# Dividing attention outputs instead of probabilities by the softmax sums, and moving six steps of a modulation vector one sub-layer ahead

## The chip, the core and the metric

The kernel runs on one core of a Trainium2 chip. The metric is the device time of one execution in microseconds (us), as a median over runs. The core has five engines that run side by side and meet at semaphores: PE (TensorE, matmuls; PEld is its weight loading), DVE (VectorE), ACT (ScalarE), POOL (GpSimd) and SP (SyncE, which here only issues DMAs). Each engine takes its own instructions strictly in order.

## The reference

Two layers of a decoder on 256 tokens of width 1024. Each layer is a half-step SwiGLU, a token mixer, and another half-step SwiGLU. Layer 0 mixes with the forgetting attention ("fox"), layer 1 with the dilated attention ("dil"). Each of the six sub-layers begins with an RMS norm that is shifted and scaled, and ends with a gate; shift, scale and gate are vectors computed from `c`.

```python
mod = (silu(c) @ mod_w[i] + mod_b[i]).reshape(B, 3, 3, D)    # 3 sub-layers x (shift, scale, gate)
...
h = modulate(rms_norm(x, norm_g[i, 1]), shift[:, 1], scale[:, 1])
...
# fox, for each of 16 heads of 64, queries in two blocks of 128:
logits = q @ k.T * scale + cum[q] - cum[k]          # masked causally
p = softmax(logits)                                  # exp(logits - max) / sum
o = p @ v
# dil, three groups of windows, merged by their softmax sums, so that one softmax runs over all of them
...
x = x + gate[:, 1] * (o @ w_out)
```

## The kernel before, in words

Everything is computed on two token tiles of 128 (`t` = 0, 1). Weights come in as f32, and each weight tile (128 x 1024) is split into two parts: ACT rounds it (`wh`, L206), DVE subtracts (`wl`, L215). A product is then three matmuls (`mm3`, L394 to L396, or `mm_blocks`, L389 to L391). PE's and SP's instructions stand in the order in which the program text emits them; those of DVE, ACT and POOL are ordered by a scheduler when the kernel is built.

The text walks through the weight tiles and calls `tick()` about every 1.4 us of PE work. At a tick, `weights.advance()` splits further tiles ahead of their use, and events that were booked with `at(delay, fn)` fall due, in order of their tick. Attention is emitted in this way, between the projections' matmuls.

**Attention** (`attention`, L902) handles a group of four heads in eight steps (head `i`, token tile `t`). `scores` emits the logits on PE, the row maximum on DVE (`lo`, `nm`, L916) and the exponential on ACT (L918), which also adds up the rows into `sums`. One tick later `share` (L922) takes the reciprocal of a sum (L926) and multiplies the row's probabilities by it (L927), both on DVE. `turn` (L929) then transposes the probabilities on PE (L935), ACT copies them to `pt` (L937), and `values` (L940) multiplies them with `v` into one PSUM bank `ob` (L948), in which the heads' outputs stand transposed. `close` (L950) splits `ob` into `oTh` (ACT) and `oTl` (DVE, L954), the operands of the output projection. There are four groups in fox and four in dil; in the last one of dil, `close` runs once for each token tile.

**Modulation vectors** (`Mods`, L256). A vector of 1024 is computed in eight steps, each of which loads 512 KB of `mod_w` into one of two buffers `mraw` and multiplies and adds it into `acc` on DVE (L296). After the eighth step the vector is split and summed over the partitions by matmuls with ones (L346, L348), into one of three tiles `mod0` (shift), `mod1` (scale), `mod2` (gate). A `Pump` (L361) spreads a sub-layer's steps evenly over its weight tiles; what is left is emitted in `flush` (L378), just ahead of the last four tiles of the output projection. In the first SwiGLU (`ffnA`) 24 steps run: its own gate and the shift and scale of fox. In fox another 24 run, the first eight of them for fox's gate.

**Boundary** (L414). At the end of a sub-layer DVE multiplies a token tile's output by the gate (`gy`, L431), adds it to `x` (L435), multiplies by the next scale (`u`, L451), and, after ACT's squares and POOL's root (`rs`, L411), finishes the next input (L460), which PE transposes (L469) for the next sub-layer. Two token tiles follow each other, and PE fills in the other's matmuls meanwhile.

**Fox** also computes the forget gates' running sums: from the `v` projection's extra columns DVE and ACT make `fl` (L1051 to L1070), which PE sums up (L1081) into `ncum` before the first logits.

Of the kernel before, what the change touches and what calls it, by code (L numbers as in the profile page):

```python
# [9 lines left out]
F32 = mybir.dt.float32  # L10
# [7 lines left out]
P = 128  # L18
# [35 lines left out]
LAST_CUTS = (0, 512, 768, 1024)  # L54
PUMP_FFN = 48
PUMP_FOX = 32
PUMP_DIL = 80
# [5 lines left out]
AHEAD = 5  # L63
SHARE = 1
QUIET0 = 5
# [26 lines left out]
def trunk_kernel(ctx, tc, x_in, c_in, positions, mod_w, mod_b, norm_g, w_gate, w_up, w_down,  # L92
# [163 lines left out]
    class Mods:  # L256
# [30 lines left out]
        def run(self):  # L287
# [12 lines left out]
            if k == 0:  # L300
                self.bias(self.done - 1 + KT)
            elif k == 2:
                dst = main.tile([P, D], F32, tag=f"mod{j}", name=f"mod{j}")
                if j == 1:
                    nc.sync.dma_start(dst, dram(norm_g, (l * 3 + s) * D, [[0, P], [1, D]]))
                mods[v] = dst
            elif k == KT - 1:
                self.finish(v, acc)

        def finish(self, v, acc):  # L310
# [50 lines left out]
    class Pump:  # L361


        def __init__(self, vectors, units):
            self.n, self.units, self.done, self.seen = len(vectors) * KT, units, 0, 0

        def __call__(self):
            self.seen += 1
            self.go(min(self.n, -(-self.n * self.seen // self.units)))

# [7 lines left out]
        def flush(self):  # L378
            while self.done < self.n or vectors.open:
                self.go(self.n)  # L380
                tick()
# [206 lines left out]

    def ffn(l, i, s, pool, n_first, new_mods, permute=False, opening=None):
        pump = Pump(new_mods, PUMP_FFN)  # L590
        weights.spare = pool, 1, "xwh", "xwl"
# [310 lines left out]
    def attention(g, first, gap, delays, pv_first, logits, mask, vblk, oTh, oTl, done, pool, width, pts_n, by_tile=False):  # L902
# [18 lines left out]

        def share(i, t):  # L922

            n, _ = mask(t)
            ri = pool.tile([P, 1], F32, tag="ri", bufs=4, name="ri")
            dve.reciprocal(ri, sums[:, t, i:i + 1])  # L926
            dve.tensor_scalar(pts[i, t][:, 0:n], pts[i, t][:, 0:n], ri, None, op0=OP.mult)  # L927

        def turn(i, t):  # L929
# [19 lines left out]

        def close(ts):  # L950
            ks = slice(2 * g, 2 * g + 2)
            for t in range(ts.start, ts.stop):
                act.copy(oTh[t][:, ks, :], ob[0][:, :, t, :])
                dve.tensor_sub(oTl[t][:, ks, :], ob[0][:, :, t, :], oTh[t][:, ks, :].bitcast(F32))  # L954
                done.update(((2 * g, t), (2 * g + 1, t)))

        for s, (i, t) in enumerate(steps):
            base = first + s * gap
            at(base, lambda i=i, t=t: scores(i, t))
            at(base + SHARE, lambda i=i, t=t: share(i, t))  # L960
            at(base + delays[0], lambda i=i, t=t: turn(i, t))
            end = max(pv_first + s * gap, base + sum(delays))
            if i % 2:
                at(end, lambda i=i, t=t: values(i, t))
            if by_tile and i == HG - 1:
                at(end, lambda t=t: close(slice(t, t + 1)))
# [66 lines left out]
    def fox(l, pool, n_first):  # L1033
        pump = Pump(MODS_FOX, PUMP_FOX)
        weights.spare = pool, 2, "qs", "ks"
# [3 lines left out]
        oTl = [pool.tile([P, KT, P], F32R, tag=f"oTl{t}", name=f"oTl{t}") for t in range(NT)]  # L1039
        fl = pool.tile([P, NT, CUM], F32, name="fl")  # L1040
        nc.gpsimd.memset(fl, 0.0)
# [81 lines left out]
        def do_heads(g):  # L1123
            attention(g, FOX_FIRST[g], 1, (T_FOX, PV_FOX), 0, *heads(g, *qkT[g]), oTh, oTl, done, pool, S, 6)

# [240 lines left out]
    with tc.tile_pool(name="ffnA", bufs=1) as fp:  # L1366
        vectors.start()
        spread_out(12, fox_tables())
        ffn(0, 0, 0, fp, 0, MODS_A, opening=opening)
    with tc.tile_pool(name="fox", bufs=1) as ap:  # L1370
# [42 lines left out]
```

## Time and profile before

| what | value |
|---|---|
| median of 3 runs | 1244.7 us (1244.12 to 1245.76) |
| the profiled execution's own time | 1244.32 us |
| span of its trace | 1242.3 us |
| mean granted PE clock | 0.996 of full speed |
| instructions in the trace | 21040 |

The trace covers the span from the first to the last instruction; the execution's own time is 2.0 us longer. Rows of the trace are in a section below. In each, a line such as L927 is the line of the code above, `out<-in` are the tiles, `x32` is a count, and what stands behind a bar or in brackets is the idle time of the engine before these instructions and what ended it.

### The profile page before, as it was taken

Reading aid. Unit: us, or ns where it says so; the run is one execution under the profiler, and the core shown is the slowest. Engines: PE = TensorE matmul, PEld = TensorE weight load, DVE = VectorE, ACT = ScalarE, POOL = GpSimd, SP = SyncE. Lnnn points to the kernel's source line nnn. Section 1 sums busy time; section 2 is a strip of 40 time slices with the busy share of each in tenths; the row PEclk is TensorE's granted clock in tenths of the full one; section 3 lists DMA queues with packets and bytes.
Section 4 is the critical chain, followed back from the end, with each engine's and each line's share of the span. In section 5 each row is a group of like instructions: output and inputs, shape, how many; then the busy total and the mean of one; then the engine's idle time right before and its main releaser. Section 6 shows DMA issues by size and latency. Waiting matters only on the chain.

```text
span 1242.3 us, 21040 instructions
## 1 busy us (share of the span) xinstructions
PE 1208.2 (97%) x8098; PEld 1082.3 (87%) x8098; DVE 965.5 (78%) x1452; ACT 660.6 (53%) x1000; POOL 96.4 (8%) x124
## 2 busy tenths in 40 slices
PE   5999999978999999999999999999999999999998
PEld 5999988866779999889999888878788787999987
DVE  7879777999988888569987669988787877765653
ACT  4446444667754555444554436566565655544440
POOL 1000000212010000000000003121131200000000
PEclk8999999999999999999999999999999999999999
DMA  9879885785749988638888647746545652867561
GB/s 334 277 271 333 284 329 159 227 277 169 228 132 317 342 275 323 207 117 285 294 289 316 214 153 237 223 158 208 176 152 171 202 172 85 270 207 220 169 207 47
DMA packets 152067, 281.18 MB, mean 226 GB/s; under 512 B 13424, under 2 KB 79504, under 8 KB 151968
## 3 DMA queue, kind: packets, MB, share of 16 engines
q1 hardware_dynamic: 151968, 279.85, 67.9%
q8 instruction: 63, 1.03, 0.3%
q14 instruction: 36, 0.29, 0.1%
HBM read 277.71 MB, written 2.10 MB: 225 GB/s over the span
## 4 chain that ended last, share of the span: by engine, by line
PE 86%; DVE 6%; ACT 2%; issue 2%; DMA 2%; POOL 1%; SPq 0%; POOLq 0%; DVEq 0%; ACTq 0%
PE bank L394 14%; PE bank L395 13%; PE bank L396 13%; PE block_bank L391 13%; PE block_bank L389 12%; PE block_bank L390 12%; PE obank L948 1%; DVE wl L215 1%; PE bank L935 1%; PE bank L1293 1%; POOL hrs L860 1%; PE bank L1288 1%; DVE acc L296 1%; PE bank L469 1%; PE bank L346 1%
## 5 line engine op out<-in xcount | busy, mean ns | idle before, releaser
L215 DVE TENSOR_TENSOR wl<-raw,wh 128x1024 fp32r<-128x1024 f32 (+1 forms) x360 | 434.9, 1215 | 156.2 <-ACT wh L206 152.7
L206 ACT CAST wh<-raw 128x1024 fp32r<-128x1024 f32 (+1 forms) x360 | 374.4, 1046 | 316.9 <-PE bank L396 118.1
L389 PE MATMUL block_bank<-hTh,wh 128*128 128x256 f32 x1312 | 371.8, 283 | 3.3 <-ACT hTh L783 3.3
L391 PE MATMUL block_bank<-hTh,wl 128*128 128x256 f32 x1312 | 371.6, 283 | 0.0
L390 PE MATMUL block_bank<-hTl,wh 128*128 128x256 f32 x1312 | 370.6, 282 | 0.0
L389 PEld LDWEIGHTS block_bank<-hTh,wh 128*128 128x128 f32 x1312 | 248.5, 189 | 3.7 <-ACT hTh L783 3.4
L390 PEld LDWEIGHTS block_bank<-hTl,wh 128*128 128x128 f32 x1312 | 248.1, 189 | 0.5 <-DVE hTl L786 0.2
L391 PEld LDWEIGHTS block_bank<-hTh,wl 128*128 128x128 f32 x1312 | 247.8, 189 | 0.0
L394 PE MATMUL bank<-wh,hTh 128*128 128x512 f32 (+2 forms) x496 | 191.1, 385 | 0.0
L396 PE MATMUL bank<-wh,hTl 128*128 128x512 f32 (+2 forms) x496 | 181.9, 367 | 0.0
L395 PE MATMUL bank<-wl,hTh 128*128 128x512 f32 (+2 forms) x496 | 181.7, 366 | 0.0
L296 DVE SCALAR_TENSOR_TENSOR acc<-mraw,ccols,acc 128x1024 f32<-128x1024 f32 x112 | 143.2, 1279 | 20.1 <-DMA mraw<-in_mod_w_dram 19.7
L395 PE MATMUL bank<-wl,aTh 128*128 128x512 f32 (+1 forms) x420 | 146.4, 349 | 0.0
L394 PE MATMUL bank<-wh,aTh 128*128 128x512 f32 (+1 forms) x420 | 146.1, 348 | 0.0
L396 PE MATMUL bank<-wh,aTl 128*128 128x512 f32 (+1 forms) x420 | 145.7, 347 | 0.0
L396 PEld LDWEIGHTS bank<-wh,hTl 128*128 128x128 f32 x496 | 93.6, 189 | 16.7 <-DVE hTl L471 0.5
L394 PEld LDWEIGHTS bank<-wh,hTh 128*128 128x128 f32 x496 | 93.8, 189 | 15.9 <-issue 1.0
L395 PEld LDWEIGHTS bank<-wl,hTh 128*128 128x128 f32 x496 | 94.0, 189 | 12.2
L394 PEld LDWEIGHTS bank<-wh,aTh 128*128 128x128 f32 x420 | 79.5, 189 | 10.9
L396 PEld LDWEIGHTS bank<-wh,aTl 128*128 128x128 f32 x420 | 79.3, 189 | 10.5
L395 PEld LDWEIGHTS bank<-wl,aTh 128*128 128x128 f32 x420 | 79.5, 189 | 10.1
L918 ACT ACTIVATE lo<-lo,nm 128x128 f32<-128x128 f32 (+1 forms) x64 | 37.8, 591 | 39.8 <-DVE nm L916 39.2
(215 smaller groups left out, 1304.4 us busy)
## 6 DMA issues: line engine op xcount, KB each, us to landing
mraw<-in_mod_w_dram SPq DMA_DIRECT2D x128, 512.0 KB, 5.1
raw<-in_ffn_w_down_dram SPq DMA_DIRECT2D x88, 512.0 KB, 3.7
raw<-in_ffn_w_gate_dram SPq DMA_DIRECT2D x76, 512.0 KB, 4.1
raw<-in_ffn_w_up_dram SPq DMA_DIRECT2D x76, 512.0 KB, 4.7
raw<-in_dil_w_in_dram SPq DMA_DIRECT2D x128, 256.0 KB, 4.1
raw<-in_fox_w_in_dram SPq DMA_DIRECT2D x36, 256.0 KB, 5.0
oraw<-in_mod_w_dram SPq DMA_DIRECT2D x32, 256.0 KB, 6.4
raw<-in_ffn_w_gate_dram SPq DMA_DIRECT2D x24, 256.0 KB, 5.1
```

What stands on the lines that cost most here:

```text
L206: act.copy(wh, self.raws[self.hi])
L215: dve.tensor_sub(wl, self.raws[self.lo], wh.bitcast(F32))
L296: dve.scalar_tensor_tensor(acc, raw, ccol[:, k:k + 1], self.bias_tile if k == 0 else acc, op0=OP.mult, op1=OP.add)
L346: pe.matmul(bp, ones, ah, start=True, stop=al is None)
L389: pe.matmul(out_i, wh[:, blk], hTh[:, :, k, :], start=first and i % 2 == 0, stop=False)
L390: pe.matmul(out_i, wh[:, blk], hTl[:, :, k, :], start=False, stop=False)
L391: pe.matmul(out_i, wl[:, blk], hTh[:, :, k, :], start=False, stop=last and i % 2 == 1)
L394: pe.matmul(o, ah, wh, start=first, stop=False)
L395: pe.matmul(o, ah, wl, start=False, stop=False)
L396: pe.matmul(o, al, wh, start=False, stop=last)
L469: pe.transpose(tp[:, k, :], self.u[h][:, k * P:(k + 1) * P], ident)
L918: act.activation(lo[:, 0:n], lo[:, 0:n], AF.Exp, bias=nm, scale=-1.0, accum_out=sums[:, t, i:i + 1])
```

## The change

`share` is gone: the exponentials go to `turn` and `values` undivided. `close` takes one reciprocal for the whole group, lets ACT spread it over 64 columns for each head (`wide`, 128 x 512), and one tick later `normalize` transposes that on PE (32 transposes in all, four for each group) into a bank `rbank`, copies it to `on` (ACT), multiplies `ob` by it (DVE), and splits `on` into `oTh` and `oTl` as before. `wide` uses the buffer of the norm's squares (`sq`), and in fox `on` that of `fl`. In fox one buffer of `pt` goes (6 to 5).

Six of the eight steps of fox's gate vector move to `ffnA`: its pump runs 30 steps over 58 units (24 over 48 before), and fox's 18 over 32. So that the gate of `ffnA` isn't overwritten, a vector's tile is now taken at its last step.

```diff
+PUMP_A = 58
+MORE_A = 6
...
-SHARE = 1
+RI_DELAY = 1
...
-        def __init__(self, vectors, units):
-            self.n, self.units, self.done, self.seen = len(vectors) * KT, units, 0, 0
+        def __init__(self, vectors, units, more=0, less=0):
+            self.n, self.units, self.done, self.seen = len(vectors) * KT - less, units, 0, 0
+            self.more = more
...
-            self.go(min(self.n, -(-self.n * self.seen // self.units)))
+            self.go(min(self.n + self.more, -(-(self.n + self.more) * self.seen // self.units)))
...
-            while self.done < self.n or vectors.open:
-                self.go(self.n)
+            while self.done < self.n + self.more or vectors.open > (self.more > 0):
+                self.go(self.n + self.more)
...
-        def share(i, t):
-
-            n, _ = mask(t)
-            ri = pool.tile([P, 1], F32, tag="ri", bufs=4, name="ri")
-            dve.reciprocal(ri, sums[:, t, i:i + 1])
-            dve.tensor_scalar(pts[i, t][:, 0:n], pts[i, t][:, 0:n], ri, None, op0=OP.mult)
...
         def close(ts):
+            ri = pool.tile([P, NT, HG], F32, tag="ri", bufs=2, name="ri")
+            dve.reciprocal(ri[:, ts], sums[:, ts])
+            wide = pool.tile([P, NT, HG, HD], F32, tag="sq", name="wide")
+            act.copy(wide[:, ts], ri[:, ts, :, None].to_broadcast([P, ts.stop - ts.start, HG, HD]))
+            at(RI_DELAY, lambda: normalize(ts, wide))
+
+        def normalize(ts, wide):
+            rb = ps.tile([P, HG // 2, NT, P], F32, tag="bank", bufs=8, name="rbank")
+            for pair in range(HG // 2):
+                for t in range(ts.start, ts.stop):
+                    cols = wide[:, t, 2 * pair:2 * pair + 2, :].rearrange("p a b -> p (a b)")
+                    pe.transpose(rb[:, pair, t, :], cols, ident)
+            on = pool.tile([P, HG // 2, NT, P], F32, tag="on", name="on")
+            act.copy(on[:, :, ts], rb[:, :, ts])
+            dve.tensor_mul(on[:, :, ts], ob[0][:, :, ts], on[:, :, ts])
             ks = slice(2 * g, 2 * g + 2)
             for t in range(ts.start, ts.stop):
-                act.copy(oTh[t][:, ks, :], ob[0][:, :, t, :])
-                dve.tensor_sub(oTl[t][:, ks, :], ob[0][:, :, t, :], oTh[t][:, ks, :].bitcast(F32))
+                act.copy(oTh[t][:, ks, :], on[:, :, t, :])
+                dve.tensor_sub(oTl[t][:, ks, :], on[:, :, t, :], oTh[t][:, ks, :].bitcast(F32))
...
-            at(base + SHARE, lambda i=i, t=t: share(i, t))
...
-        pump = Pump(MODS_FOX, PUMP_FOX)
+        pump = Pump(MODS_FOX, PUMP_FOX, less=MORE_A)
...
-            attention(g, FOX_FIRST[g], 1, (T_FOX, PV_FOX), 0, *heads(g, *qkT[g]), oTh, oTl, done, pool, S, 6)
+            attention(g, FOX_FIRST[g], 1, (T_FOX, PV_FOX), 0, *heads(g, *qkT[g]), oTh, oTl, done, pool, S, 5)
...
-        ffn(0, 0, 0, fp, 0, MODS_A, opening=opening)
+        ffn(0, 0, 0, fp, 0, MODS_A, opening=opening, units=PUMP_A, more=MORE_A)
```

The change also moves instructions, as the built programs' orders show. The first place is the Boundary from `ffnA` to fox, on DVE. Before, from the first `gy` to the end of the first token tile's input:

```order
L431 TENSOR_TENSOR gy<-bank,mod_911 128x512
L435 TENSOR_TENSOR x_83<-x_83,gy 128x512
L451 TENSOR_TENSOR u<-x_83,mod_1996 128x512
L431 TENSOR_TENSOR gy<-bank,mod_911 128x512
L435 TENSOR_TENSOR x_83<-x_83,gy 128x512
L451 TENSOR_TENSOR u<-x_83,mod_1996 128x512
L407 SCALAR_TENSOR_TENSOR msq<-ss 128x1
L460 SCALAR_TENSOR_TENSOR u<-u,rs,mod_1486 128x512 x2
```

With the change (lines are those of the changed file, as in all rows of it here; L298 is a modulation step):

```order
L298 SCALAR_TENSOR_TENSOR acc<-mraw,ccols,acc 128x1024
L438 TENSOR_TENSOR gy<-bank,mod_1237 128x512
L442 TENSOR_TENSOR x_83<-x_83,gy 128x512
L298 SCALAR_TENSOR_TENSOR acc<-mraw,ccols,acc 128x1024
L458 TENSOR_TENSOR u<-x_83,mod_1975 128x512
L438 TENSOR_TENSOR gy<-bank,mod_1237 128x512
L298 SCALAR_TENSOR_TENSOR acc<-mraw,ccols,acc 128x1024
L442 TENSOR_TENSOR x_83<-x_83,gy 128x512
L438 TENSOR_TENSOR gy<-bank,mod_1237 128x512
L458 TENSOR_TENSOR u<-x_83,mod_1975 128x512
L414 SCALAR_TENSOR_TENSOR msq<-ss 128x1
L467 SCALAR_TENSOR_TENSOR u<-u,rs,mod_1788 128x512 x2
```

Two steps now stand inside this chain, and the second token tile's first `gy` stands ahead of the first tile's last `u`.

The second place is the end of a group of heads in dil, on PE, with the change (before, the row of L962 isn't there and the rest is the same). Names: `obank` is `ob`, `rbank` the transposed reciprocals.

```order
L948 MATMUL obank<-pt,v_8895 64x128 x4
L948 MATMUL obank<-pt,w_8980 64x128 x2
L401 MATMUL bank<-wh,hTh 128x512
L402 MATMUL bank<-wl,hTh 128x512
L403 MATMUL bank<-wh,hTl 128x512
L401 MATMUL bank<-wh,hTh 128x512
L402 MATMUL bank<-wl,hTh 128x512
L403 MATMUL bank<-wh,hTl 128x512
L962 MATMUL rbank<-ident,wide 128x128 x4
```

Six matmuls of a projection, one tick, stand between the last `values` and the new transposes; in fox it is more, except at its last group, where the transposes follow the last `values` at once, ahead of four matmuls of a modulation vector:

```order
L948 MATMUL obank<-pt,v_3796 64x128 x4
L948 MATMUL obank<-pt,v_3797 64x128 x2
L962 MATMUL rbank<-ident,wide 128x128 x4
L351 MATMUL bank<-wh,ones 128x512
L353 MATMUL bank<-wl,ones 128x512
```

Before, the matmuls with ones followed the last `values` directly. In fox, DVE's order has 13 large instructions (weight splits and modulation steps) from the first split of fox's `v` weights (128x544) to the forget gates' first instruction before, and 12 with the change; from there to `fl` it has 7 in both. From `ncum` to the end of the last group 16 modulation steps stand before and 12 with the change. On PE, the four matmuls with ones of fox's gate vector now stand ahead of L1081, no longer behind it.

## Rows read from the trace of the kernel before

**Rows 1.** Part 1 of the page: busy time of each engine.

```profile
PE 1208.2 (97%) x8098; PEld 1082.3 (87%) x8098; DVE 965.5 (78%) x1452; ACT 660.6 (53%) x1000; POOL 96.4 (8%) x124
```

**Rows 2.** Busy time by stretch: PE, PEld, DVE, ACT, POOL, clock, DMA share.

```profile
150.00:200.00 50.00, 50.00 (x279) 43.55 (x278) 36.52 (x32) 25.04 (x26) 0.00 (x0) 1.00 0.81 289
218.00:257.00 39.00, 33.09 (x195) 28.58 (x194) 35.28 (x56) 24.80 (x43) 5.92 (x6) 0.98 0.80 253
257.00:349.00 92.00, 82.36 (x529) 65.03 (x528) 84.04 (x209) 68.81 (x176) 18.11 (x24) 0.99 0.68 219
...
795.00:1055.00 260.00, 257.92 (x1523) 208.30 (x1523) 209.51 (x391) 157.73 (x272) 40.53 (x38) 1.00 0.54 172
```

**Rows 3.** What PE waited for: us in total, times, longest.

```profile
PE bank L935 <- DVE lo L927: 10.2, 13, 1.6
...
PE bank L1081 <- DVE fl L1070: 4.4, 1, 4.4
...
PE bank L890 <- DVE qn L864: 1.6, 1, 1.6
PE obank L948 <- DVE oTl L954: 1.1, 1, 1.1
```

**Rows 4.** DVE's groups in 257 to 349: busy us, mean ns, idle before.

```profile
L215 DVE TENSOR_TENSOR wl<-raw,wh 128x1024 fp32r<-128x1024 f32 x19 | 23.1, 1217 | 0.1
L296 DVE SCALAR_TENSOR_TENSOR acc<-mraw,ccols,acc 128x1024 f32<-128x1024 f32 x14 | 17.8, 1273 | 1.5 <-DMA mraw<-in_mod_w_dram 1.5
...
L927 DVE TENSOR_SCALAR lo<-lo,ri 128x128 f32<-128x128 f32 (+1 forms) x32 | 10.0, 315 | 0.1
...
L926 DVE RECIPROCAL ri<-sums 128x1 f32<-128x1 f32 x32 | 4.9, 155 | 1.2 <-ACT lo L918 1.1
```

**Rows 5.** PE's groups in 795 to 1055 (dil): the transposes of probabilities.

```profile
L935 PE MATMUL bank<-ident,lo 128*128 128x128 f32 x128 | 19.7, 276 | 0.7 <-DVE lo L927 0.7
```

**Rows 6.** Tile `mod`: ns min/median/max, first and last start, forms.

```profile
L431 DVE TENSOR_TENSOR gy<-bank,mod x28: 411/682/692, 207.1 to 1238.6; 128x512 f32<-128x512 f32 x20, 128x256 f32<-128x256 f32 x8
...
L354 ACT COPY mod<-bank x14: 587/593/606, 157.7 to 938.2; 128x512 f32<-128x512 f32 x14
```

**Rows 7.** PE alone, by the microsecond and in one later stretch: busy, clock.

```profile
255.00:256.00 1.00, 1.00 (x5) 0.57 0.95 373
256.00:257.00 1.00, 1.00 (x4) 0.50 1.08 380
257.00:258.00 1.00, 1.00 (x6) 0.50 1.08 394
258.00:259.00 1.00, 1.00 (x5) 0.72 0.99 358
270.00:280.00 10.00, 7.89 (x49) 1.00 0.87 283
```

**Rows 8.** DVE in order of time, Boundary from `ffnA` to fox: start, us.

```profile
208.53 0.69 DVE L451 TENSOR_TENSOR u<-x,mod 128x512 f32<-128x512 f32 x1
209.79 0.69 DVE L431 TENSOR_TENSOR gy<-bank,mod 128x512 f32<-128x512 f32 x1 [0.58 <-PE bank L396]
...
212.83 1.42 DVE L460 SCALAR_TENSOR_TENSOR u<-u,rs,mod 128x512 f32<-128x512 f32 x2 [0.67 <-POOL rs L411]
```

**Rows 9.** PE in order of time, same Boundary: start, us.

```profile
213.39 0.28 PE L394 MATMUL bank<-wh,aTh 128*128 128x256 f32 x1
...
213.75 0.60 PE L469 MATMUL bank<-ident,u 128*128 128x128 f32 x4
214.10 0.36 PE L394 MATMUL bank<-xwh,aTh 128*128 128x256 f32 x1
...
214.55 0.28 PE L394 MATMUL bank<-wh,aTh 128*128 128x256 f32 x1
```

**Rows 10.** Part 6 of the page: KB each, median us to landing.

```profile
mraw<-in_mod_w_dram SPq DMA_DIRECT2D x128, 512.0 KB, 5.1
```

**Rows 11.** ACT's weight splits in 257 to 349.

```profile
L206 ACT CAST wh<-raw 128x1024 fp32r<-128x1024 f32 x19 | 19.9, 1048 | 2.6 <-PE bank L396 2.5
```

More of the change, by code (lines that the diff above doesn't have):

```diff
@@ L301, in run, with target @@
                 self.bias(self.done - 1 + KT)
[L302 to L306, printed above, removed]
+            elif k == 2 and j == 1:
+                self.target(v)
+                nc.sync.dma_start(mods[v], dram(norm_g, (l * 3 + s) * D, [[0, P], [1, D]]))
             elif k == KT - 1:
+                if j != 1:
+                    self.target(v)
                 self.finish(v, acc)
+        def target(self, v):
+            mods[v] = main.tile([P, D], F32, tag=f"mod{v[2]}", name=f"mod{v[2]}")
         def finish(self, v, acc):
@@ L587, in plan_ffn, with ffn @@
         plan_out(NF, w_down[l, i], SPARE_FFN)
-    def ffn(l, i, s, pool, n_first, new_mods, permute=False, opening=None):
-        pump = Pump(new_mods, PUMP_FFN)
+    def ffn(l, i, s, pool, n_first, new_mods, permute=False, opening=None, units=PUMP_FFN, more=0):
+        pump = Pump(new_mods, units, more)
         weights.spare = pool, 1, "xwh", "xwl"
@@ L1039, in fox @@
         oTl = [pool.tile([P, KT, P], F32R, tag=f"oTl{t}", name=f"oTl{t}") for t in range(NT)]
-        fl = pool.tile([P, NT, CUM], F32, name="fl")
+        fl = pool.tile([P, NT, CUM], F32, tag="on", name="fl")
         nc.gpsimd.memset(fl, 0.0)
```

## The prediction

> **What bounds the kernel now.** I began with the engines' busy times over the whole span [rows 1]: PE is busy 97% of it, so a gain must come out of the few places where PE stands still, and whatever the change adds to PE is paid in full. Next came the stretches in which attention runs [rows 2]. In dil, PE is busy 257.9 of 260 us. In fox it isn't: from 218 to 257 it is idle for 5.9 of 39 us, and from 257 to 349, where its heads are computed, for 9.6 of 92. In that second stretch DVE is busy 84.0 of 92 us (91%) and ACT 68.8 (75%): there DVE is the engine that sets the pace. PE's waits say the same [rows 3]. The transposes of the probabilities (L935) wait 10.2 us in 13 pieces, each ended by `share`'s multiplication (L927), and of this only 0.7 us lies in dil [rows 5], so 9.5 us lie in fox. One wait of 4.4 us is for `fl`, one of 1.6 us for a norm; both lie before 257. After the long one PE ran at 1.2 GHz for most of four microseconds: granted 0.57, 0.50, 0.50 and 0.72 of 2.4 GHz [rows 7], a loss of 0.43 + 0.50 + 0.50 + 0.28 = 1.7 us. The waits of up to 1.6 us in 270 to 280, which leave PE busy for only 7.9 of 10 us, left the clock at 1.00 [rows 7].
>
> **The change, part by part.**
>
> *Removed from DVE.* In fox 32 multiplications of 315 ns and 32 reciprocals of 155 ns: 10.0 + 4.9 = 14.9 us, all in 257 to 349 [rows 4]. In the same stretch four modulation steps fewer (16 to 12) of 1.27 us: 5.1 us. Added for three groups whose products fall into it: a reciprocal (0.16) and a 128x512 product out of PSUM, for which the nearest row is `gy` at 0.68 us [rows 6], so 3 x 0.84 = 2.5 us. DVE's load falls from 84.0 to 66.5 us, while PE's own work there is 82.4 us. DVE stops being the bound.
>
> *What becomes of the 9.5 us.* Two neighbours bound it. In dil DVE is 81% busy (209.5 of 260) and PE loses only 0.7 us to the same wait; after the change the stretch in fox takes some 85.6 us (92, less 7.0 and 0.8 of waits and slow clock by the terms below, plus three sets of transposes at 0.45), and DVE is at 66.5 of these, 78%. That speaks for a remainder of 0.5 us. Against it stands ACT: it gets two 128x512 copies a group at 0.59 us [rows 6], about 3.5 us in this stretch, and since the stretch gets shorter it rises from 75% to 72.3 of 85.6, 84%. The exponential and the copy of `pt` now set when PE can go on, and both are ACT's; an engine at 91% cost 9.5 us here, so one at 84% could cost up to 6. Between the ends I take 2.5, nearer to dil's, since part of ACT's busy time isn't late for anybody: **7.0 us gained**, between 3.5 and 9.
>
> *The wait for `fl`.* DVE has one large instruction fewer ahead of the forget gates (12, not 13, of 1.2 to 1.3 us): 1.25 us. The second token tile's `gy` and `x` have been brought forward in the Boundary, which brings DVE about 0.6 us nearer to PE. The four matmuls with ones now stand ahead of L1081, some 0.9 us at the 0.23 us that a 512-wide matmul takes from start to start in L394's stream (three of 256 columns take 0.36 [rows 9], so one of 512 twice 0.12); PE arrives that much later, with work it had to do anyway. Of 4.4 us, 1.6 are left: **2.8 us gained**, between 0 and 4.4. A wait of 1.6 us is as short as those that left the clock alone, so the **1.7 us** of the low clock go too; if the wait stays as long as it is, they don't. The norm's wait has no part taken out of it but shares the lighter DVE: 0.4 of 1.6. Dil's 0.7 falls to 0.2, for the multiplication that ended it is gone: 0.5.
>
> *The Boundary from `ffnA` to fox.* Here the moved steps cost something. Before, the second `gy` had waited 0.58 us for PE and L460 0.67 us for POOL [rows 8]; L460's first half ended at 212.83 + 0.75 = 213.6, and PE's transposes began at 213.75 [rows 9], 0.2 us later, so the chain has next to no slack. Now a step of 1.28 us stands before the first `u`: that `u` ends at 208.53 + 1.28 + 0.69 = 210.5 instead of 209.2, so the second `gy`, which stood at 209.79, starts 0.7 us late. A second step delays `x` by another 1.28, and the other tile's `gy` ahead of the last `u` by 0.69. Together 2.6 us, less 0.2 of slack: PE, whose order is unchanged, **loses 2.5 us** at L469. Not below 1.2 (if POOL's 0.67 and the `gy`'s 0.69 are absorbed); up to 4.0 if a step also waits for its load: a load lands 5.1 us after issue [rows 10], and the last two are issued as buffers come free, 4 to 5 us before their steps. SP holds four such loads in a row, with fox's weight loads behind them; those wait for their own buffers until the Boundary is over, so I put nothing on that. The other four moved steps lie ahead of the Boundary, in `ffnA`'s output phase, where from 150 to 200 PE is busy throughout and DVE for 36.5 of 50 us [rows 2], idle between its splits: nothing, and at most their own 5.1 us if that cover were gone.
>
> *Added to PE.* 32 transposes. Four of the same form (L469) push the next matmul from 213.75 to 214.10, and the three matmuls behind them take 0.45 instead of 0.36 [rows 9]: 0.45 us for four, **3.6 us** for 32. All of it counts, since PE is what is full.
>
> *New waits at these transposes.* They need `wide`, that is a reciprocal and an ACT copy that can start before the last `values` do, as they only need the sums. One tick of projection (1.4 us) plus the `values` lie in between, more in fox; at fox's last group nothing does. At the end of dil the second tile's `values` must wait until `ob` has been read, now by the product instead of by `oTl`, which cost 1.1 us [rows 3] and may cost 0.4 more. For all of these I take **0.9 us**, from 0 to the rival's price below.
>
> *Sum.* -7.0 - 2.8 - 1.7 - 0.4 - 0.5 + 2.5 + 3.6 + 0.9 = -5.4 us. Against the profiled execution's own time of 1244.3 us that is 1238.9; that execution lies 0.4 us below the median of the runs. I say 1239.
>
> The Trainium skill, "Perfetto Trace Analysis", section "Identifying the Most-Contended Engine", would have one optimise the engine with the highest occupancy first (TensorE judged by its weight loads' busy share). Over the span that is PE, with weight loads at 87% against DVE's 78% [rows 1], and then this change loads the wrong engine; the rival that follows from it is the third below. In 257 to 349 the trace has DVE at 91% and the weight loads at 71% [rows 2], so there the rule names DVE.
>
> **Rivals.**
>
> *ACT takes DVE's place.* For it: 84% as worked out, on an engine that works in order and now holds copies that wait for PE. Then PE waits for exponentials about as long as it did for `share`; 7 of the 9.5 us stay, 4.5 more than I took: 1243.4.
>
> *PE is freed altogether.* All 9.5, 4.4 and 1.6 us of fox's waits go, with the 1.7 of the clock and 0.7 in dil; the Boundary costs 1.2 and the new waits 0.5: 1244.3 - 17.9 + 1.2 + 3.6 + 0.5 = 1231.7. Against it: the norm's wait depends on POOL, too.
>
> *PE is the bound and nothing comes back.* The waits merely change their names: +3.6 + 2.5 + 0.9 = 1251.3. For it, PE at 97% and 32 instructions more; against it, that the waits in fox end with the very instruction that is removed.
>
> *PE waits at each new set of transposes* (the slower side). If `wide` is queued on ACT behind a weight split of 1.05 us [rows 11], and behind that comes its own 0.6 and the reciprocal's 0.16, each of the nine sets makes PE wait up to 1.8 us: 16.2 us instead of 0.9, 1254.2. It decides (slower by more than 0.2%) once a set costs about 1.0 us on the mean. Against it: the tick between.
>
> **How the numbers follow.** My forecast 0.55, ACT in DVE's place 0.18, PE freed 0.15, nothing comes back 0.05, waits at the transposes 0.07. A measurement of this kernel can tell about 0.2%, 2.5 us, from no change: faster means below 1242.2. The forecast lies there but for its own worst corner (ACT and the Boundary at their dear ends), about a tenth of it, and the freed case wholly: 0.65. The ACT case, with that corner, is within 0.2%: 0.23. The last two are slower: 0.12. For the range I leave out those two at the top and the better half of the freed case at the bottom: 1233 to 1246.
>
> **What the profile would show.** Right: in fox's heads DVE at about 80%, PE's waits at L935 below 4 us and ended by ACT; the wait at L1081 at 1 to 2 us and the clock at 1.00 behind it; a new wait of about 2.5 us at the first L469 of fox; four transposes at about 0.45 us; no wait above 1 us at `rbank`. Wrong: waits at `rbank` or for `pt` of more than 8 us in sum, a clock that falls at the Boundary, or PE gaps in dil beyond the 2.1 us that are there now.

## The result and the profile after

The changed kernel takes 1250.94 us (median, 1250.51 to 1252.79) against 1245.02 for the kernel before in the same runs: the ratio is 1.0051, 95% interval 1.0033 to 1.0068. It is slower by 0.5%, where 1239.0 and "faster" were forecast; it also lies outside the range (1233 to 1246). The traced execution has a span of 1248.9 us, 6.6 more than before.

Part 1 of the page of the changed kernel, to be read beside [rows 1]:

```profile
PE 1216.8 (97%) x8130; PEld 1090.6 (87%) x8130; DVE 946.0 (76%) x1342; ACT 667.3 (53%) x1018; POOL 94.6 (8%) x124
```

DVE lost 19.5 us of work, as intended, and PE is busy for 8.6 us more, in part at the low clock. Busy time by stretch (PE, PEld, DVE, ACT, POOL, clock, DMA share), the first two at the times of [rows 2], the third up to the end of fox, the fourth all of dil:

```profile
150.00:200.00 50.00, 50.00 (x284) 43.77 (x283) 39.57 (x35) 24.02 (x26) 0.00 (x0) 1.00 0.86 296
218.00:257.00 39.00, 36.78 (x214) 32.35 (x214) 34.34 (x55) 26.38 (x47) 7.80 (x10) 0.96 0.65 199
257.00:362.00 105.00, 97.33 (x594) 77.98 (x594) 84.54 (x168) 76.35 (x190) 18.38 (x25) 0.97 0.58 195
744.00:1054.00 310.00, 306.68 (x1774) 248.97 (x1772) 239.12 (x412) 185.76 (x323) 54.73 (x50) 1.00 0.56 179
```

In fox's heads DVE is at 81% (84.5 of 105; over the same work before 95.1 of 104.7, 91%), as forecast. But the clock is at 0.97, and in dil PE stands still for 3.3 us, where over the same work it had been 1.8. What PE waited for (total, times, longest):

```profile
PE bank L935 <- ACT lo L925: 3.8, 4, 1.7
PE bank L476 <- DVE u L467: 3.3, 3, 2.8
...
PE bank L1107 <- DVE qs L905: 2.4, 2, 1.6
...
PE bank L1095 <- DVE fl L1084: 1.9, 1, 1.9
PE obank L948 <- DVE on L965: 1.2, 1, 1.2
PE bank L351 <- DVE wh L337: 1.0, 1, 1.0
PE bank L1106 <- DVE ncum L1098: 1.0, 1, 1.0
PE bank L401 <- DVE qn L871: 0.9, 1, 0.9
PE bank L897 <- DVE qn L871: 0.8, 1, 0.8
```

Against [rows 3]: the waits for probabilities fell from 10.2 to 3.8 us and are now ended by ACT, and the wait for `fl` from 4.4 to 1.9. New are the Boundary's 2.8 us (L476), 1.0 at the ones of a vector that ends inside `ffnA` (L351), and waits for results of the head norm and of the gates' sums (`qs`, `ncum`; those for `qn`, 1.7 us in two pieces, were one of 1.6 before). PE by short stretches (busy, clock), behind the Boundary and in the heads:

```profile
218.00:221.00 3.00, 3.00 (x19) 0.66 0.34 94
221.00:224.00 3.00, 3.00 (x13) 0.77 0.00 0
304.00:308.00 4.00, 2.43 (x17) 0.96 0.66 252
308.00:312.00 4.00, 3.14 (x16) 0.50 0.00 0
312.00:316.00 4.00, 4.00 (x25) 0.68 0.73 260
```

The clock that was low behind `fl` [rows 7] is full there now, but is low in these two places.

**Where the 6.6 us arose.** From the start to fox's first input transposes (213.75 in [rows 9], now 217.88): +4.1, of which the Boundary's wait is 2.8 and L351's 1.0. Fox, from there to `ffnB`'s first input transposes: 145.2 to 144.2, -1.0. Dil, taken the same way: 306.6 to 310.2, +3.6. The SwiGLUs behind: within 0.1. Fox can be split further, with idle PE time summed over windows of half a microsecond and the clock's loss as busy time times what was not granted: before, 145.20 = 15.55 idle + 1.71 clock + 127.94 work; after, 144.15 = 9.91 + 4.69 + 129.54. PE did win 5.6 us of idle time, and lost 3.0 to the clock and 1.6 to more work.

### The profile page after: what moved, and what is told of

Read it like the earlier page. It is cut to its first block, busy times and chain, and to the rows that moved or that the text cites. A ratio compares the mean times of both kernels' runs of the same rounds, so it can differ in the third digit from the quotient of the medians.

```text
span 1248.9 us, 21032 instructions
## 1 busy us (share of the span) xinstructions
PE 1216.8 (97%) x8130; PEld 1090.6 (87%) x8130; DVE 946.0 (76%) x1342; ACT 667.3 (53%) x1018; POOL 94.6 (8%) x124
## 4 chain that ended last, share of the span: by engine, by line
PE 71%; issue 19%; DVE 4%; ACT 3%; DMA 2%; POOL 1%; SPq 0%; POOLq 0%; DVEq 0%; ACTq 0%
PE bank L401 12%; PE bank L402 12%; PE bank L403 12%; PE block_bank L398 9%; PE block_bank L396 9%; PE block_bank L397 9%; PE obank L948 2%; PE bank L935 1%; DVE wl L217 1%; PE bank L1307 1%; DMA mraw<-in_mod_w_dram 1%; ACT wh L208 1%; PE bank L476 1%; PE bank L1302 1%; PE bank L885 0%
## 5 line engine op out<-in xcount | busy, mean ns | idle before, releaser
L298 DVE SCALAR_TENSOR_TENSOR acc<-mraw,ccols,acc 128x1024 f32<-128x1024 f32 x112 | 143.1, 1278 | 25.0 <-DMA mraw<-in_mod_w_dram 24.6
```

The costliest lines, as they stand in the source:

```text
L298: dve.scalar_tensor_tensor(acc, raw, ccol[:, k:k + 1], self.bias_tile if k == 0 else acc, op0=OP.mult, op1=OP.add)
```

## The experiments

All times stand as ratios to the kernel before, measured beside it; fox and dil are read from one trace each. e8, e12, e15, e16 and e18 stand in the text. "Division alone" is the changed kernel with `MORE_A = 0, PUMP_A = 48`.

| run | ratio (95%) | fox, us | dil, us |
|---|---|---|---|
| before | 1 | 145.2 | 306.6 |
| changed kernel | 1.0051 (1.0033 to 1.0068) | 144.2 | 310.2 |
| e1 division alone | 1.0026 (1.0016 to 1.0036) | 145.6 | 310.0 |
| e2 moved steps alone | 1.0027 (1.0016 to 1.0038) | 145.2 | 307.0 |
| e3 no division at all | 0.9966 (0.9954 to 0.9978) | 142.2 | 305.6 |
| e4 change, steps earlier | 1.0045 (1.0033 to 1.0058) | 142.3 | 310.5 |
| e5 e1, heads later | 1.0015 (1.0006 to 1.0024) | 143.6 | 309.8 |
| e6 e1, `wide` on POOL | 1.0032 (1.0020 to 1.0045) | 147.6 | 311.6 |
| e7 e1, no transposes | 0.9969 (0.9957 to 0.9980) | 144.1 | 304.6 |
| e9 e1, unread transposes | 0.9978 (0.9969 to 0.9987) | 142.8 | 306.2 |
| e10 e1, `ks` copy on POOL | 1.0023 (1.0014 to 1.0032) | 146.0 | 310.1 |
| e11 before, six steps left out | 0.9998 (0.9990 to 1.0007) | 144.2 | 306.7 |
| e13 e1, half the link | 1.0011 (0.9997 to 1.0025) | 142.9 | 310.1 |
| e14 e1, `RI_DELAY = 3` | 1.0052 (1.0040 to 1.0065) | 145.9 | 311.8 |
| e17 e1, `RI_DELAY = 0` | 0.9993 (0.9984 to 1.0002) | 143.6 | 307.1 |

**The two parts apart.** e1 is the changed kernel without the moved steps; e2 is the kernel before with them:

```diff
-PUMP_A = 58
-MORE_A = 6
+PUMP_A = 48
+MORE_A = 0
```

> The division alone: the six steps stay in fox, as in the kernel before. Theory A (the losses add up: the division itself is not worth its price): what the trace after shows between 257 and 362 us and in dil stays, that is 9.5 us of waits for the divided probabilities become some 6 of others, eight sets of transposes cost 0.52 us each in dil and fox, dil loses 3.6 us in all, and with a slow clock of 3.5 us in fox's heads the time is 5 us above the kernel before, without it 1.5 us above. Theory B (the steps inside the Boundary are the loss, the division gains as predicted): 3 to 4 us below the kernel before. In both the Boundary's wait of 2.8 us is gone, and the wait for fl is back at about 4.4 us with the clock at 0.50 behind it.

> The moved steps alone: six steps of fox's gate vector in ffnA, probabilities divided as in the kernel before. Theory A: the Boundary loses 2.8 us of waiting, 1.4 of slow clock and up to 1.0 for a wait at the vector's end inside ffnA, and gets back 2.4 of the wait for fl and 1.7 of slow clock, so about 1 us slower; four steps fewer in the heads (5.1 us of DVE) may bring 1 to 2 us, so between 1 us faster and 1.5 slower. Theory B: 4 to 6 us slower, as what the Boundary delays isn't made good later.

Each part costs about 3.3 us, and together they cost about the sum. So theory B, by which the division gains and only the Boundary loses, is wrong. Theory A has e1 between its two values (1.5 and 5), but e2's 3.4 us lie between the ranges of both theories: it gave back less than A allowed. In e2 the wait for `fl` is 1.9 us, with a full clock, but ten microseconds on PE stands still for probabilities (in order of time: start, duration):

```profile
268.48 0.47 PE L941 MATMUL bank<-ident,lo 128*128 128x128 f32 x1 [3.58 <-DVE lo L933]
```

**e4** spreads the 30 steps over 50 units, so that none stands inside the Boundary's chain.

```diff
-PUMP_A = 58
+PUMP_A = 50
```

> The changed kernel with its 30 steps of ffnA spread over 50 units instead of 58, so that the last of them stands ahead of the Boundary's first product and none inside it. Theory A: the Boundary's wait of 2.8 us and the 1.4 us of slow clock behind it go, 4 us of the 6 us that the change lost; 1.5 to 2.5 us above the kernel before. Theory B: 3 to 5 us below the kernel before, for then all of the predicted gain shows. Against both: the steps come earlier, where the DMA share is 0.8 to 0.97, and their loads may delay weights; that would show as waits of ACT for raw that PE feels between 50 and 200 us.

The Boundary's wait went as expected, but nothing was gained: another one grew in its place. PE in order of time:

```profile
106.55 0.83 PE L351 MATMUL bank<-wh,ones 128*128 128x512 f32 x2 [3.05 <-DVE wh L337]
```

The vector's sum now comes due before DVE has it, and the clock is at 0.50 behind it. The time is 5.6 us above the kernel before; neither theory had this.

**e11** leaves six steps out of the kernel before (`less=6`, and the list of steps without them).

> The kernel before, with six of the eight steps of fox's gate vector left out altogether, their loads too (the vector is then a partial sum): what moving them could bring at most, if ffnA took them for nothing. The prediction's theory: 2.8 us of the wait for fl and the 1.7 us of slow clock behind it, and 1 to 3 us of the waits for divided probabilities: 5 to 7 us below the kernel before. Theory E (the shorter wait for fl is given back, since PE then comes to the first heads sooner than DVE and ACT have their work done, as in the moved steps alone, where a wait of 3.6 us stands 10 us behind fl): 0.5 to 3 us below.

Theory E holds in kind, and even more is given back than it said: the wait for `fl` is 1.9 us here too, a wait of 3.6 for probabilities follows, and the time doesn't change. Leaving six steps out of fox won nothing that can be measured.

**e3** leaves the division out (no `share`, nothing in its place).

```diff
-            at(base + SHARE, lambda i=i, t=t: share(i, t))
```

> The kernel before without any division: the reciprocals and multiplications of share are left out and nothing takes their place, so the outputs stay unnormalised; steps as in the kernel before. It prices what the removal alone is worth. The prediction's theory: 7.0 to 7.5 us faster, for the waits in fox's heads go from 9.5 to 2.5 us and dil's 0.7 to 0.2. Theory A: PE's waits move on to other results of DVE and ACT (qs, qn, ncum, pt, the exponentials), so 2 to 4 us faster. If a slow clock shows up in the heads here too, without any new instruction on PE, it is the pattern of PE's waits that brings it and not the transposes.

4.2 us faster, near theory A's 2 to 4. As an estimate that is the most that a cheaper division could bring, if the order of the other instructions stays as good as here. PE's idle time in fox falls from 15.6 to 11.8 us only: waits of 3.1 us for `qs` and 1.2 for `qn` take over. Windows of e3 in fox's heads (columns as above):

```profile
271.00:286.00 15.00, 13.12 (x77) 9.74 (x77) 13.91 (x28) 11.42 (x29) 2.07 (x3) 1.00 0.76 252
286.00:301.00 15.00, 14.34 (x92) 10.95 (x91) 13.81 (x28) 10.97 (x34) 2.65 (x2) 1.00 0.63 212
...
316.00:331.00 15.00, 12.91 (x92) 10.39 (x93) 13.76 (x29) 14.67 (x38) 0.00 (x0) 1.00 0.76 262
```

Even without any division DVE is 92 to 93% busy from 271 to 301 us, and ACT 98% from 316 to 331. The forecast had averaged over 92 us. The clock is at 1.00 in these windows: no low clock showed up in e3's heads behind the one at `fl`.

**e7 and e9: what the transposes cost.** Both copy `on` from `wide` unturned, so the outputs are divided by the wrong numbers. e7 has no transposes; e9 has 32 of a constant that nobody reads.

```diff
-            act.copy(on[:, :, ts], rb[:, :, ts])
+            act.copy(on[:, :, ts], wide[:, ts].rearrange("p t (c a) b -> p c t (a b)", c=HG // 2))
...
+                    pe.transpose(rb[:, pair, t, :], ident, ident)
```

> The division alone without its 32 transposes: the spread reciprocals are copied to on unturned, so that the outputs are divided by the wrong numbers; all of ACT's and DVE's instructions stay. It prices PE's share. Theory A (PE pays them in full): 4.1 us faster than the division alone (dil grew by 2.07 us beyond its waits for 16 of them), that is about 1244.3, and dil about 307.5 to 308. Rival (the transposes stand in idle time of PE, and what costs is the waits around them): less than 1.5 us faster.

> The division alone without the turning of the reciprocals (1240.95 us, 7.5 below the division alone), but with 32 transposes of a constant at the same places, into the same bank, which nobody reads. It separates PE's own work from the chain that runs through it. Theory A' (the new instructions are paid for twice, as work on PE and by the dependences that pass through PE, from wide to the transposes to ACT's copy): PE's work alone, 32 x 0.13 to 0.15 us, about 4.5 us, so 1245 to 1246, and PE idles in dil less than 1 us. Rival (what costs is that the transposes shift everything else on PE, dependences or not): the full 7.5 us, 1248 to 1249, with the same 3 us of idle time in dil. Second rival (they stand in time that PE has free): below 1243.

Without transposes the division costs nothing against e3. As bare work they add 1.6 us to dil, 0.40 for each set of four, and about 1.1 us to the whole, with intervals that overlap: in time e9 comes out where the second rival put it, below 1243. The real transposes cost some 7 us (1.0026 against 0.9969). So six parts in seven lie in something that comes with their links to the other engines, and dil has 3.8 us of it (310.0 against 306.2).

**e13 and e14** look for the link. In e13 PE reads `wide`, but `on` doesn't come from PE; e14 is `RI_DELAY = 3`.

> The division alone, with the transposes of wide at their place but unread: on is copied from wide itself (so the outputs are divided by unturned reciprocals). PE still waits for wide, but ACT's copy of on, DVE's product and the split no longer wait for PE. With the transposes read by nobody and reading a constant the kernel took 1241.4 us, with both links 1248.4. Theory F (what costs is the link from PE to ACT: a copy at the head of ACT's queue that waits for PE, and with it exponentials, weight splits and DVE behind it): 1241 to 1243. Rival G (what costs is PE's own wait for wide, and with it everything behind it on PE): 1246.5 to 1249.

> The division alone with normalize three ticks behind close instead of one (4.2 us of projection instead of 1.4 between the last values and the transposes). Theory F: nothing is gained for ACT's copy, which stands directly behind the transposes as before: within 1 us of 1248.4. Rival G: PE's link to wide gets 2.8 us of slack, so 2 to 5 us faster, 1243.5 to 1246.5. Should it be a question of which instructions the schedulers of DVE and ACT put around the copies, either may come out.

Both theories fail in dil: in e13 it is as long as in e1, though PE waits at no transpose and ACT's copy waits for none, and a longer delay makes it longer (e14 is 3.2 us slower than e1, as neither theory had it). In the whole time e13 lies at the edge of rival G's range; its fox is 2.7 us shorter than e1's in one trace each, and whether the link costs something there is open. Another candidate is the order of DVE's instructions around the head norm. The kernel before, DVE in order of time at the end of dil's first group:

```profile
850.92 0.69 DVE L857 TENSOR_REDUCE hms<-sq 128x8 f32<-128x512 f32 x1
851.85 1.23 DVE L215 TENSOR_TENSOR wl<-raw,wh 128x1024 fp32r<-128x1024 f32 x1 [0.25 <-ACT wh L206]
853.00 0.42 DVE L954 TENSOR_TENSOR oTl<-obank,oTh 128x256 fp32r<-128x256 f32 x1
853.53 0.48 DVE L880 TENSOR_SCALAR qT<-bank,gain 128x256 f32<-128x256 f32 x1
853.93 0.68 DVE L864 TENSOR_TENSOR qn<-bank,hrs 128x512 f32<-128x512 f32 x1
```

The changed kernel, the same place:

```profile
855.90 0.75 DVE L969 TENSOR_TENSOR oTl<-on,oTh 128x256 fp32r<-128x256 f32 x2
856.57 0.48 DVE L887 TENSOR_SCALAR qT<-bank,gain 128x256 f32<-128x256 f32 x1
856.96 0.67 DVE L864 TENSOR_REDUCE hms<-sq 128x8 f32<-128x512 f32 x1
858.21 0.69 DVE L871 TENSOR_TENSOR qn<-bank,hrs 128x512 f32<-128x512 f32 x1 [0.57 <-POOL hrs L867]
860.28 0.69 DVE L871 TENSOR_TENSOR qn<-bank,hrs 128x512 f32<-128x512 f32 x1 [1.38 <-POOL hrs L867]
```

Between the second sum (`hms`) and the first `qn`, before, stand a weight split, a half of the outputs' split and `qT`, and POOL's root is ready by the time they are done. Now `qn` follows bare and DVE stands still for POOL. The Trainium skill, "PSUM — Partial Sum Buffer", section "Engine vs sequencer instructions", has the queues of ScalarE, VectorE and GpSimdE as strict FIFO; the trace agrees, for the 1.38 us hold up everything that stands behind.

**e17** books `normalize` in the tick of `close`. That puts a weight split and `qT` back between the sum and the first `qn`, with the real division in place (DVE in e17, the same place):

```profile
849.51 0.69 DVE L864 TENSOR_REDUCE hms<-sq 128x8 f32<-128x512 f32 x1
850.45 1.23 DVE L217 TENSOR_TENSOR wl<-raw,wh 128x1024 fp32r<-128x1024 f32 x1 [0.25 <-ACT wh L208]
851.59 0.48 DVE L887 TENSOR_SCALAR qT<-bank,gain 128x256 f32<-128x256 f32 x1
851.98 0.68 DVE L871 TENSOR_TENSOR qn<-bank,hrs 128x512 f32<-128x512 f32 x1
```

The edit:

```diff
-RI_DELAY = 1
+RI_DELAY = 0
```

> The division alone with normalize booked for the tick of close itself instead of one later, so that the transposes follow the last values at once. In dil this also gives DVE its old order around the head norm back: before, two weight splits and two products for keys (qT) stand between the norm's sum (hms) and qn, which needs POOL's root; in the division alone qn follows hms with nothing or one small instruction between them, and DVE waited for the root 16.3 us in 13 pieces instead of 10.3 in 7. Theory H (in dil the loss beyond PE's own work is this order of DVE's): DVE's waits for hrs in dil fall to 10 to 12 us, dil to 306.5 to 308 from 310.0, and the time by 2 to 3.5 us to 1245 to 1246.5. Rival G (PE's wait for wide): the transposes now come before wide is ready, waits at rbank of 0.5 to 1.5 us each, nine sets, so 1251 or more.

Theory H's figures for dil came: it is 307.1 us, 2.9 less than in e1, and PE waits 1.2 us in it instead of 3.1. That is 1.9 of the 2.9 us; the other 1.0 is busy time of PE, for which the transposes' new place may account. The whole is 4.1 us faster than e1 by the ratios (0.0033 of 1245), more than H's 3.5; fox is 2.0 us shorter in the traces, with 1.7 us lost to the clock instead of 4.5. Rival G is out: at `rbank` PE waits 0.9 us once in fox, and not at all in dil. DVE's waits in dil, in the changed kernel:

```profile
DVE acc L298 <- DMA mraw<-in_mod_w_dram: 18.2, 8, 3.6
DVE qn L871 <- POOL hrs L867: 16.4, 13, 2.1
```

and in e17:

```profile
DVE acc L298 <- DMA mraw<-in_mod_w_dram: 15.3, 7, 3.6
DVE qn L871 <- POOL hrs L867: 11.6, 9, 2.1
```

Over the kernel before, the changed one and the experiments but e8, the two lots don't overlap: where DVE waits 10.3 to 11.6 us for the root, dil takes 304.6 to 307.1 us; where it waits 16.3 to 18.3, dil takes 309.8 to 313.8. But DVE's waits for the loads of modulation steps part the same lots (9.6 to 15.3 us against 16.9 to 23.1), so the lots alone don't say which wait counts. The changed kernel's waits for exponentials in dil (0.9, 0.5 and 0.8 us), none of which e17 has, say more. The longest, on DVE, ACT and PE:

```profile
878.62 1.28 DVE L298 SCALAR_TENSOR_TENSOR acc<-mraw,ccols,acc 128x1024 f32<-128x1024 f32 x1 [1.50 <-DMA mraw<-in_mod_w_dram]
879.83 0.68 DVE L923 CUSTOM_DVE_ANT_0 lo<-bank,table 128x512 f32<-128x512 f32 x1
880.55 0.72 ACT L925 ACTIVATE lo<-lo,nm 128x512 f32<-128x512 f32 x1 [3.73 <-DVE nm L923]
881.42 0.66 PE L935 MATMUL bank<-ident,lo 128*128 128x128 f32 x4 [0.92 <-ACT lo L925]
```

The row maximum (L923) stands behind a step that waited for its load, and ACT and PE wait for it. The second piece has a step that waited 1.7 us ahead of it, the third a `qn` that waited 2.1 us for POOL. Counted from dil's first transposes, the step above began at 134.6 us; before it began at 130.5 and in e17 at 129.8, and there no exponential came late, though it waited for its load as well (3.5 us in both). So behind the head norm DVE as a whole runs late, and PE feels it through whatever stands ahead of the next row maximum. How the order at the norm makes the load come later was not followed, and as `RI_DELAY = 0` also moves the transposes on PE, the order isn't isolated by e17 alone; e13 is what speaks against PE's part.

**Smaller ones.** e5 begins fox's heads one tick later (`FOX_FIRST = (18, 8, 8, 8)`), e16 does so in the kernel before, e10 puts the second `ks` copy on POOL, e12 does so in the kernel before, and e6 puts `wide` there.

> The division alone, with the heads of fox's groups 1 to 3 begun one tick (1.4 us of projection) later. In the division alone PE waits 2.7 us in three pieces for qs, with no division at all 3.1 us in two: results of the head norm's chain that the waits for divided probabilities used to cover. Theory C (the gain in fox's heads fell short because PE runs into this second chain, whose length doesn't change): the waits for qs fall below 0.5 us, PE idles 2 to 3 us less between fl and the end of fox, and the time is 1 to 2.5 us below the division alone's 1248.4. Rival (ACT's load is what holds PE): the waits only turn into waits for exponentials, and the time stays within 1 us of 1248.4.

> The kernel before with the heads of fox's groups 1 to 3 begun one tick later, nothing else changed. If the waits in fox's heads are a matter of DVE's load (it is 96% busy from 270 to 285 us), starting later moves them and the time stays within 1.5 us of the kernel before. If they are a matter of the chain from the head norm to the first logits, it gains 1.5 us or more here too, and then the 1.5 us that the later heads brought to the division are no property of the division.

> The division alone, with the second copy of the keys' high parts (ks, 64x256, 16 in fox) on POOL instead of ACT. In the stretch of 15 us in which the keys of fox's last group are prepared, 316 to 331 us, ACT is busy for 14.7 of 15 us in the division alone, 14.7 with no division at all and 14.6 before. Theory D (ACT is the bound in that stretch and DVE, at 94 to 96% from 271 to 301, in the other, so that averages over the whole of fox hid both): PE idles about 1 us less there, the time is 0.5 to 2 us below the division alone's 1248.4. Rival (the idle time is the length of a chain, not an engine's load): no change beyond 0.5 us, or a loss of 1 to 3 us because POOL's copy takes longer than ACT's 0.4.

> The kernel before with the same copy of the keys on POOL. Theory D: ACT isn't what its heads wait for (DVE's multiplication is), so within 1 us of the kernel before; a gain of 1 us or more would say that ACT's load already held PE there. Rival: 1 to 3 us slower by POOL's longer copy.

> The division alone, with the spreading of the reciprocals to wide moved from ACT to POOL, which is busy 8% of the span: nine copies of about 0.6 us off ACT. If ACT's extra copies are what makes PE wait in dil (2.1 us for exponentials in three pieces, none of them there with no division at all), dil gets 1 to 2 us shorter than the 310.0 us of the division alone and the time falls to 1246.5 to 1247.5. If they aren't, dil stays within 0.5 us, or gets longer by new waits at the transposes of wide, as POOL needs longer for a copy.

e5: the waits for `qs` went, but waits for exponentials took their place (6.0 us, 3.2 in e1), and PE's idle time in fox stayed (11.1 us, 10.7 in e1). The 1.4 us by which e5 lies below e1, with intervals that overlap, came in the traces with the clock (2.7 lost, not 4.5), so theory C falls on the idle time, though its range for the time was met. e16 is 1.0014 (1.0005 to 1.0023), 1.7 us slower: no gain there. e10 is unclear, 0.4 us below e1 within overlapping intervals; in its 315 to 330 us ACT is at 13.9 of 15, so theory D's relief is small at best. e12 is 0.9995 (0.9987 to 1.0004), no difference. e6 made dil longer, not shorter: with the copies off ACT, PE's waits for exponentials in dil rose from 1.8 to 3.3 us, so those copies' load wasn't what held PE there. POOL's copy of 128x512 took no longer than ACT's (0.62 us each), and no wait at the transposes came of it in dil.

e8 has `share`'s multiplications on POOL in the kernel before, and is 1.0199, 24.8 us slower, more than the 20 that were thought of. Its group on POOL:

```profile
L927 POOL TENSOR_SCALAR lo<-lo,ri 128x128 f32<-128x128 f32 (+1 forms) x64 | 88.1, 1378 | 191.7 <-DVE ri L926 153.2 <-PE bank L396 20.7 <-PE bank L1094 6.9
```

1.38 us on the mean, where DVE took 0.40 for the same 64 in the kernel before (a 128x256 took 1.40 on POOL and 0.35 on DVE); PE waited 27.2 us for them.

> The kernel before with share's multiplications on POOL instead of DVE; reciprocals and steps as they were. With no division at all the kernel was 3.8 us faster, which bounds what any cheaper division can bring. Theory C: DVE loses the same 10 us in fox as in the change, PE's waits for the divided probabilities fall, and no instruction is added to PE or ACT: 1 to 3 us below the kernel before, if POOL needs less than about a microsecond for 128x256. If it needs longer, or if POOL and DVE slow each other down, the waits at the transposes of the probabilities grow in both attentions and the time is 2 to 20 us above the kernel before.

> A version meant to be the best of the division: normalize three ticks behind close, heads of fox one tick later, the second copy of the keys on POOL. The later heads brought 1.5 us and the copy on POOL 0.5 by themselves. If these add up and the delay brings nothing: 1246.5; if the delay removes the links' cost: 1242 to 1244, below the kernel before (1244.4 to 1245.5).

> The same with fox's heads of groups 1 to 3 one tick later, which brought the division alone 1.5 us: the last candidate. If both effects add up, 1243.5 to 1245, level with the kernel before or 1 us below it; a division that beats the kernel before by more than 0.2% is not expected by either theory, since even with the transposes as bare work it was 2.7 us below.

e18 is 0.9997 (0.9988 to 1.0006), inside the expected range, but not below e17: the two effects don't add up. e15 (delay 3, later heads and `ks` on POOL together) is 1.0079, 9.8 us slower and far from both times expected. No version that divides rightly beats the kernel before by what can be measured; the best division, e17, is level with it. The full change with `RI_DELAY = 0` was not run.

## Why the prediction was wrong

The forecast was -5.4 us, the traces show +6.6: 12.0 us to explain.

*What becomes of the 9.5 us* failed, and with 6.3 us it is the largest part. From the sums of the gates to `ffnB`'s first transposes the terms came to some -6.5 us (-7.0, -1.7 for the clock, four sets of transposes, a share of the new waits), and the traces show 104.7 and 104.5 us. The term itself was too large: with nothing put in the division's place (e3), this stretch's trace is 2.6 us shorter and the whole 4.2 us faster, not 7.0. That `share`'s waits would go was right: L935's in fox fell from 9.5 to 1.7 us. But idle time fell by 2.5 us only (9.7 to 7.2) and the clock's loss rose by 1.3 (1.7 to 3.0), as it fell in a new place. The step took dil, at 81%, as the neighbour for a stretch whose average would be 78%; but this stretch has parts in which DVE (92 to 93%) or ACT (98%) is all but full even without a division (e3). That these parts are what turns up the next waits is read from the windows and was not tested by itself. The Trainium skill, "Perfetto Trace Analysis", section "Optimization Strategy", speaks of kernels with several regimes, between which the most contended engine changes; the windows of e3 agree, and the step had taken one regime for all.

*The wait for `fl`* was sized rightly (1.9 us left, 1.6 forecast, a full clock behind it), but counted as a gain. It is given back at the next wait (in e2 and e11 of 3.6 us, for probabilities). With the low clock behind the Boundary, fox ahead of its heads won 0.9 us, not 3.2.

*The Boundary* was right: 2.8 us (2.5 forecast). What was not forecast, and listed as what would prove it wrong, is the clock behind it. And the other four steps, costed at nothing, made the vector's end in `ffnA` wait 1.0 us.

*New waits at the transposes* failed in its view, not only its size. It looked for waits on PE at `rbank`, and there were none above 1 us, as forecast. Two things came in its place: the split comes a tick later, a `qn` that had cover has none, and DVE runs late behind it; and dil's 0.7 us of waits for probabilities, which were to fall to 0.2, became 2.1 us of waits for exponentials. The terms for dil made +1.7 us, measured are 3.6; with the booking of e17 2.9 us of e1's loss in dil go. That the delay of a tick costs this is shown, the way through DVE's order is read from the traces. PE's gaps in dil also passed the 2.1 us that the prediction had named as a sign of being wrong.

*The transposes* were about right in dil (0.40 for four, 0.45 forecast).

The rival "PE is the bound and nothing comes back" gave 1251.3 us, close to the result, by luck and for other reasons: PE as the bound would have made e9 dear, and it cost little. By the Trainium skill's rule that this rival leaned on ("Perfetto Trace Analysis", section "Identifying the Most-Contended Engine") the sign comes out right; the loss doesn't come from the load on that engine. "ACT takes DVE's place" describes some 15 us of fox (316 to 331), but not dil, where ACT stood idle until DVE's row maximum came (for 3.7 us in the rows above).

**Open.** Single traces vary. From the start to fox's first input transposes seventeen of the kernels have the same instructions to run, and their traces take 213.5 to 214.9 us; executions of the kernel before lie between 1243.3 and 1247.2 us. In dil, kernels with the same instructions there lie closer together: 306.6 to 307.0 us in four without the new division (the kernel before, e2, e11, e16), 309.8 to 310.5 in four with it (the changed kernel, e1, e4, e5). So dil's 3 us are no chance, but of fox's differences of 1 to 2 us between single traces a part may be. The clock takes part in that: behind a wait of 4.2 to 4.4 us for `fl` it cost 1.7 us in the kernel before, 2.8 in e1 and 1.6 in e3. Which waits bring the clock down is not settled.

## What to carry over

Divide a stretch until each piece has one full engine before judging what relieving an engine brings; an average of 80% can be made of pieces at 95%. When a step is moved or delayed, read on every in-order engine what stood between a producer and its consumer and now doesn't: here a tick's delay took the cover from a root on another engine, and undoing the delay brought more (4.1 us) than the bare transposes cost (about 1.1). A wait made shorter early in a busy stretch is no gain until the next wait behind it has been read too.

## What the runs showed of the hardware

Transposes that nobody waits for are cheap in a full stream of matmuls: the rows of e9 show 0.28 us for one, but 16 of them made dil 1.6 us longer, 0.10 each. The granted clock fell to 0.50 of 2.4 GHz (1.2 GHz) at 219.0 us behind a wait of 2.8 us at the Boundary, and at 307.7 us behind waits of 0.1 and 1.6 us that ended at 303.8 and 305.9; behind the wait of 1.9 us for `fl` it stayed at 1.00 (all in the changed kernel). POOL took 0.9 to 1.6 us for the multiplications of 128 to 512 columns for which DVE took 0.3 to 0.5 (e8 and the kernel before).
